# The norm's root in steps between VectorE's long instructions, and five small moves in a two-layer decoder trunk

## The chip, the cores and the metric

The kernel runs on one core of a Trainium2 chip. The metric is the device time of one launch in microseconds. TensorE multiplies, VectorE and ScalarE do the elementwise work and move results out of the accumulators, GpSimd (POOL) issues the DMAs that add to what lies in memory, and SyncE (SP) issues the other DMAs. Each engine works through its own instructions in the order in which the program gives them.

## The reference, cut to what matters

The input x has 512 tokens of 1024 values in float32. Two layers follow; a layer is a gated feed-forward part, a mixing part and a second feed-forward part, each added to x:

```python
for l in range(DEPTH):                                   # 2 layers
    x = x + 0.5 * swiglu(rmsnorm(x, ln_ffn1[l]), w_ffn1_gu[l], w_ffn1_down[l])
    h = rmsnorm(x, ln_mix[l])
    z = h @ w_in[l]                                      # pool, q, k, v, two gates
    ...                                                  # windowed means, attention over 128 tokens
    x = x + (g_pool * a + g_attn * b) @ w_out[l]
    x = x + 0.5 * swiglu(rmsnorm(x, ln_ffn2[l]), w_ffn2_gu[l], w_ffn2_down[l])

def rmsnorm(x, g):  return x * rsqrt(mean(x * x, axis=-1) + 1e-6) * g
def swiglu(h, w_gu, w_down):
    g, u = split(h @ w_gu, 2)                            # 1024 -> 2 x 2816
    return (silu(g) * u) @ w_down                        # 2816 -> 1024
```

The four feed-forward parts (FFNs) hold most of the arithmetic, and the change is in them.

## The kernel before, in words

**Two parts of every number.** Float32 operands are split into a high part that TensorE multiplies at its faster float32 rate and a low part, the rest. A product is three matmuls: high by high, high by low, low by high. ScalarE makes a high part by a rounding copy (`wh` for weights, `xgh`, `more` or `op` for activations), VectorE the low part by a subtraction (`wl`, `xgl`, `more`, `op`). For weights `Weights` (line 168) keeps a plan of tiles of up to 1024 columns: loads run up to 7 tiles ahead, high parts 4 and low parts 3. `prep` (line 295), called once for each tile that is used up, emits the next low part, the next sum of two weight tiles (`add_up`), the next high part and the loads that have a free buffer. A load that is a difference or sum of two tiles is a DMA by SP and an accumulating DMA by POOL.

**Fewer products.** `strassen` (line 551) computes a 2 x 2 block product with seven products instead of eight. Its stages come in the order `a11, s1, s2, a12, s3, s4, a22`. Their activations are combinations of the four blocks: a11 takes B11, s1 takes T1, s2 takes T2, a12 takes B21, s3 takes T3, s4 takes B22, a22 takes T4. The banks A, C and Dd of the accumulators are shared: a11, s2, s3 and a22 add up in A, s1 and s4 in C, a12 in Dd. A stage has two weight tiles (c = 0, 1), and in each two halves of the tokens (q = 0, 1). Behind c = 0 comes a `prep`, behind c = 1 the stage's own step, which moves the bank out, then `settle()`, then another `prep`. `settle` (line 148) emits the low parts that were put off. `mid` names extra work at (stage, c, q): there `settle()` is called and then the entry.

**An FFN** (line 530) has three groups of columns, one of 2 x 384 and two of 2 x 512. In each group two blocks (`block`, line 592) compute gate and up, and `down` (line 765) multiplies by the down weights and adds to x. The first block's results are turned by TensorE through the bank `pt` (`turned`, line 667) in the second block's a11 step, and become down's first operands, for its stages a11 and s1: `made` emitted the high and the low part there. In `down`, the results of a11 and s1 are copied to the tiles `p` and `u` (`aside`) and added to x by POOL's accumulating DMAs (`gathered`); the other stages are added to x by VectorE.

**The norm.** `Norm.sums` (line 480) makes the variance (`rs_v`) and its inverse root by a bit trick and three Newton rounds (`rsqrt`, line 330): two instructions and three times three, on tiles of 128 x 4 values, each of which reads the result of the one before. For an FFN the negative (`nrstd`) follows. The first block of an FFN behind a norm begins its matmuls with the scaled but not yet normed x; the root is needed only by the activations in a12's step and called for in s2's step. At the same time the last two transposed pieces of x come in, and the combinations T2 to T4 are made, by a list of ten pieces of work (`left`, line 522) that `due` takes one by one at entries of `mid` (lines 870 to 875).

**The very first block** is `plain` (line 700): eight weight tiles, in two passes j = 0 and 1 of four (c). VectorE makes the combinations T1 (`first`, four) and T2 to T4 (`other`, four) behind the matmuls of each c, ahead of each `other` ScalarE makes a scaled copy `xg`, and behind j = 0, c = 3 come the root and four Silu activations of the finished pass. The group's second block then runs `strassen`.

All of this is emitted by hand in this order. Since every instruction is recorded at one helper (line 97), the profile's rows are told apart by the tiles' names.

Of the kernel before, what the change touches and what calls it, by code (L numbers as in the profile page):

```python
# [12 lines left out]
I32 = mybir.dt.int32  # L13
# [7 lines left out]
S = 512  # L21
# [87 lines left out]
def trunk(ctx, tc, x0, xT, consts, vecs, rows, w_g4, w_g3, w_d8, w_d6, w_qkv, w_u, w_pool, w_gate, w_br, w_out, out):  # L109
# [36 lines left out]
    unsettled = []  # L146

    def settle():
        while unsettled:
            unsettled.pop(0)()  # L150

# [16 lines left out]
    class Weights:  # L168
# [77 lines left out]
        def add_up(self, upto):  # L246

            while self.summed < len(self.plan):
# [3 lines left out]
                if c["of"] is not None:  # L252
# [12 lines left out]
                    b["uses"] -= 1  # L265
                self.summed += 1
# [8 lines left out]
        def low(self, upto):  # L275
            while len(self.lo) < min(upto, len(self.hi)):
# [6 lines left out]
                c["uses"] -= 1  # L283

# [45 lines left out]
    def rsqrt(y, v):  # L330

        t = sp.tile(list(v.shape), F32, name="rs_t%d" % math.prod(v.shape[1:]))
        nc.vector.tensor_scalar(
            out=y.bitcast(I32), in0=v.bitcast(I32), scalar1=1, scalar2=None, op0=ALU.logical_shift_right
        )
        nc.vector.tensor_scalar(
            out=y.bitcast(I32), in0=y.bitcast(I32), scalar1=-1.0, scalar2=float(0x5F3759DF),
            op0=ALU.mult, op1=ALU.add,
        )
        for _ in range(3):  # L340
            nc.vector.tensor_tensor(out=t, in0=y, in1=y, op=ALU.mult)
            nc.vector.scalar_tensor_tensor(out=t, in0=t, scalar=-0.5, in1=v, op0=ALU.mult, op1=ALU.mult)
            nc.vector.scalar_tensor_tensor(out=y, in0=t, scalar=1.5, in1=y, op0=ALU.add, op1=ALU.mult)
# [4 lines left out]
    class Norm:  # L348
# [92 lines left out]
        def others(self, j, src, xg, scale):  # L441
# [4 lines left out]
            )  # L446
            nc.vector.scalar_tensor_tensor(
                out=t[:, :HT], in0=src[:, :HT], scalar=scale, in1=t[:, HT:], op0=ALU.mult, op1=ALU.subtract
            )
            nc.vector.scalar_tensor_tensor(  # L450
                out=u, in0=t[:, :HT], scalar=-1.0, in1=xg[:, :HT], op0=ALU.mult, op1=ALU.subtract
            )
            split(*self.of(T2, j), t[:, :HT])
# [26 lines left out]
        def sums(self, acc=None, pt=None):  # L480
# [11 lines left out]
            rsqrt(self.rstd, v)  # L492
            if self.halves:
                self.nrstd = xp.tile([P, NB], F32, name="nrstd")
                nc.vector.tensor_scalar(out=self.nrstd, in0=self.rstd, scalar1=-1.0, scalar2=None, op0=ALU.mult)
                return
            hi, lo = sp.tile([P, NB], F32R, name="rs_h"), sp.tile([P, NB], F32, name="rs_l")
# [32 lines left out]
    def ffn(ctx, nm, nxt, last):  # L530
# [20 lines left out]
        def strassen(order, n, sizes, operand, steps, mid={}):  # L551
# [8 lines left out]
            for kind in order:  # L560
# [3 lines left out]
                for c, kn in enumerate(sizes):  # L564
                    wh, wl = (t[:, :kn * n].rearrange("p (k f) -> p k f", k=kn) for t in W.take(kind))
                    for q in range(2):
                        for k in range(kn):
                            ah, al = operand(kind, k0 + k, q)
                            for j, (s, m) in enumerate(((ah, wh), (ah, wl), (al, wh))):
# [3 lines left out]
                                )  # L573
                        if (kind, c, q) in mid:
# [17 lines left out]
        def block(n, i, order, mid):  # L592
# [10 lines left out]
            def s1(pt):  # L603
                tile_["p"] = wide("p")[:, :, :n]
                nc.scalar.copy(out=tile_["p"], in_=pt)

            def s2(pt):
# [3 lines left out]
                if nm.rstd is None:  # L611
                    nm.sums()

            def a12(pt):
                nc.vector.tensor_tensor(out=r, in0=r, in1=pt, op=ALU.add)
# [47 lines left out]
        def made(name, src, n):  # L663
            high(name, src, n)
            low(name)

        def turned(src, i, t, n):
# [10 lines left out]
            elif i == 0:  # L678
                made("a11", pt, n)
                f["a"] = fp.tile([P, 2, S], F32, name="fa")[:, :, :n]  # L680
                nc.vector.tensor_tensor(out=f["a"], in0=pt, in1=f["b"], op=ALU.subtract)
                made("s1", f["a"], n)
# [17 lines left out]
        def plain(n, xt, acc, later):  # L700
# [17 lines left out]

            def other(j):
                xg = temp("xg")  # L720
                nc.scalar.activation(out=xg, in_=part(j + 4), func=AF.Copy, scale=nm.gain[:, j + 4:j + 5])
                nm.others(j, part(j), xg, ngain[:, j:j + 1])
# [4 lines left out]
            for j in range(2):  # L727
                pts = [t[:, q, :n] for t in ((A, C) if j == 0 else (Dd, turn)) for q in range(2)]
                for c in range(4):
# [19 lines left out]
                    if j == 0 and c == 3:  # L749
                        for h, name in enumerate(("r1", "u")):  # L750
                            act.append(wide(name)[:, :, :n])
                            for q in range(2):
                                nc.scalar.activation(
                                    out=act[h][:, q, :], in_=pts[2 * h + q], func=AF.Silu, scale=rs(2 * h + q)
# [10 lines left out]
        def down(n, final):  # L765
# [21 lines left out]
            def aside(t, d, c, pt, name):  # L787
                half = wide(name)
                nc.scalar.activation(out=half, in_=pt, func=AF.Copy, scale=c)
                pend_x.append((x[:, 2 * t:2 * t + 2, d * S:(d + 1) * S], half))  # L790

            def gathered():
                y, half = pend_x.pop(0)
                nc.gpsimd.dma_start(out=y, in_=half, accum_op=ALU.add)
# [3 lines left out]
            def a11(pt):  # L798
                aside(0, 0, 0.5, pt, "p")
# [556 lines left out]
```

## Time and profile before

| | |
|---|---|
| time, median of 3 runs | 1876.44 us (1876.26 to 1877.54) |
| time of the profiled execution | 1876.08 us |
| its span, first to last instruction | 1874.3 us |
| TensorE matmuls | 1854.3 us busy, 99% of the span, 8928 |
| VectorE | 1421.7 us, 76% |
| ScalarE | 1029.8 us, 55% |
| GpSimd | 152.0 us, 8% |
| mean granted TensorE clock | 1.000 |

A row of the timeline gives the start in microseconds from the span's start, the duration, the engine (PE is TensorE, DVE VectorE, ACT ScalarE), the operation, the tiles written and read, the shapes, and in brackets the idle time ahead of it with what ended it. Consecutive rows of one kind are merged (x2). A matmul's row lasts longer than the distance to the next, since matmuls overlap; the pace is read from start to start.

### The profile page before, as it was taken

What the parts mean: (1) busy time and instruction counts of PE and PEld (TensorE: products, weight loads), DVE (VectorE), ACT (ScalarE), POOL (GpSimd) and SP (SyncE); (2) the same over time, 40 slices, a digit from 0 to 9 for tenths busy, and PEclk for the clock granted to TensorE, in tenths of its full rate; (3) what the DMA queues carried; (4) which work ended last, traced back from release to release, by engine and by line L of the source; (5) the groups of instructions that cost most, each with busy time, mean ns of one, the idle gap of its engine ahead of it and who ended that gap; (6) DMA issues with size and microseconds to landing.
All of it is one profiled execution on the core that took longest, in us unless ns stands there. A gap on an engine that the chain in (4) does not pass through costs nothing.

```text
span 1874.3 us, 23990 instructions
## 1 busy us (share of the span) xinstructions
PE 1854.3 (99%) x8928; PEld 1556.8 (83%) x8928; DVE 1421.7 (76%) x1805; ACT 1029.8 (55%) x1517; POOL 152.0 (8%) x176
## 2 busy tenths in 40 slices
PE   9999999999999999999999999999999999999998
PEld 8888888887788789988878898888877887899887
DVE  7878878677563977887898878786675648888877
ACT  6655555645444655555665555565554446646554
POOL 0100101000000001110101111110000001101000
PEclk9999999999999999999999999999999999999999
DMA  8786867322223677687767768763222237677864
GB/s 252 190 243 180 218 175 190 131 79 77 82 90 102 167 201 184 180 227 193 193 167 197 173 180 230 199 183 107 90 68 90 93 87 213 169 192 179 241 180 124
DMA packets 94100, 305.39 MB, mean 163 GB/s; under 512 B 10240, under 2 KB 10496, under 8 KB 93984
## 3 DMA queue, kind: packets, MB, share of 16 engines
q1 hardware_dynamic: 67104, 223.47, 35.1%
q0 software_dynamic: 26736, 80.37, 24.5%
q8 instruction: 70, 1.15, 0.2%
q14 instruction: 46, 0.38, 0.1%
q10 hardware_dynamic: 144, 0.03, 0.0%
HBM read 289.15 MB, written 2.10 MB: 155 GB/s over the span
## 4 chain that ended last, share of the span: by engine, by line
PE 84%; DVE 8%; ACT 5%; issue 2%; DMA 1%; SPq 0%; DVEq 0%; POOL 0%; ACTq 0%
PE mm L97 77%; PE sc L97 4%; DVE wl L97 2%; PE pt L97 2%; ACT wh L97 2%; DVE sums L97 1%; PE pt_pv L97 1%; DVE x L97 1%; DVE more L97 1%; ACT sq L97 1%; ACT xgh L97 1%; ACT xg L97 1%; PE pt_tp L97 1%; DVE xgl L97 0%; ACT s L97 0%
## 5 line engine op out<-in xcount | busy, mean ns | idle before, releaser
L97 DVE TENSOR_TENSOR wl<-raw,wh 128x1024 fp32r<-128x1024 f32 (+3 forms) x443 | 503.8, 1147 | 95.4 <-PE mm L97 57.8
L97 ACT CAST wh<-raw 128x1024 fp32r<-128x1024 f32 (+3 forms) x443 | 433.8, 988 | 249.3 <-PE mm L97 171.8
L97 PE MATMUL mm<-wh,op 128*128 128x512 f32 x1232 | 391.6, 394 | 0.0
L97 PE MATMUL mm<-wh,more 128*128 128x512 f32 (+1 forms) x1104 | 335.0, 374 | 3.0 <-DVE more L97 3.0
L97 PE MATMUL mm<-wl,xgh 128*128 128x512 f32 (+2 forms) x840 | 310.3, 369 | 4.1 <-DVE wl L97 4.0
L97 PE MATMUL mm<-wh,xgh 128*128 128x512 f32 (+2 forms) x840 | 312.8, 372 | 0.9 <-ACT xg L97 0.7
L97 PE MATMUL mm<-wh,xgl 128*128 128x512 f32 (+2 forms) x840 | 310.2, 369 | 0.9 <-DVE xgl L97 0.9
L97 PEld LDWEIGHTS mm<-wh,op 128*128 128x128 f32 x1232 | 231.2, 188 | 48.3 <-DVE op L97 1.7
L97 PE MATMUL mm<-wl,op 128*128 128x512 f32 x616 | 240.6, 391 | 1.6 <-DVE wl L97 1.6
L97 PEld LDWEIGHTS mm<-wh,more 128*128 128x128 f32 x1104 | 204.8, 188 | 34.3 <-DVE more L97 5.0
L97 PE MATMUL mm<-wl,more 128*128 128x512 f32 (+1 forms) x552 | 206.5, 374 | 1.1 <-DVE wl L97 1.1
L97 DVE TENSOR_TENSOR wl<-sums,wh 128x1024 fp32r<-128x1024 f32 (+1 forms) x140 | 159.1, 1137 | 45.8 <-ACT wh L97 27.6
L97 ACT CAST wh<-sums 128x1024 fp32r<-128x1024 f32 (+1 forms) x140 | 136.9, 980 | 89.0 <-DVE sums L97 46.3
L97 POOL DMA_DIRECT2D raw<-in_w_g x92 | 78.5, 854 | 1265.5 <-DMA raw<-in_w_g 743.4
L97 PEld LDWEIGHTS mm<-wl,xgh 128*128 128x128 f32 x840 | 158.1, 188 | 26.9 <-DVE wl L97 6.2
L97 PEld LDWEIGHTS mm<-wh,xgl 128*128 128x128 f32 x840 | 157.9, 188 | 23.4 <-DVE xgl L97 2.2
L97 PEld LDWEIGHTS mm<-wh,xgh 128*128 128x128 f32 x840 | 158.0, 188 | 23.0 <-ACT xg L97 2.0
L97 PEld LDWEIGHTS mm<-wl,op 128*128 128x128 f32 x616 | 115.9, 188 | 26.0 <-DVE wl L97 3.3
L97 PE MATMUL mm<-xgh,wh 128*128 128x512 f32 x320 | 129.3, 404 | 0.0
L97 PE MATMUL mm<-xgl,wh 128*128 128x512 f32 x320 | 125.4, 392 | 0.5 <-DVE xgl L97 0.5
L97 PE MATMUL mm<-xgh,wl 128*128 128x512 f32 x320 | 125.3, 392 | 0.0
L97 PEld LDWEIGHTS mm<-wl,more 128*128 128x128 f32 x552 | 103.7, 188 | 17.6 <-DVE wl L97 2.4
(251 smaller groups left out, 2432.0 us busy)
## 6 DMA issues: line engine op xcount, KB each, us to landing
raw<-in_w_g SPq DMA_DIRECT2D x160, 512.0 KB, 5.2
raw<-in_w_d SPq DMA_DIRECT2D x100, 512.0 KB, 4.5
raw<-in_w_g POOLq DMA_DIRECT2D x64, 512.0 KB, 6.3
raw<-in_w_g SPq DMA_DIRECT2D x77, 384.0 KB, 4.4
raw<-in_w_d POOLq DMA_DIRECT2D x40, 512.0 KB, 5.4
raw<-in_w_gate SPq DMA_DIRECT2D x32, 512.0 KB, 3.2
raw<-in_w_g POOLq DMA_DIRECT2D x28, 384.0 KB, 5.8
raw<-in_w_br SPq DMA_DIRECT2D x16, 512.0 KB, 3.2
```

The lines of the kernel that those rows point to most:

```text
L97: return lambda *args, **kw: self.tc.keep_in_program_order(call(*args, **kw))
```

## The change

The root's twelve instructions become a list (`rsqrt_steps`). For an FFN behind a norm they aren't emitted in a row but put on a list `slow`, from which `tick` takes one behind each deferred low part and each sum of weight tiles, two behind each low part of a weight tile, and one behind each of the three combinations in `Norm.others`. What is left is emitted ahead of a12's addition, or, in `plain`, ahead of the activations. The call moves from s2's step to s1's.

The other moves: the low parts of down's first operands go from the second block's a11 step to entries at s1 (in the first group of all, s2); in down, the copies `aside` go from the ends of a11 and s1 to entries at s1 and s2, and the second accumulating DMA one entry later; in an FFN's first block, the last piece of the list goes from (s3, 1, 1) to (s4, 0, 0), and an empty entry at (a12, 1, 0) settles there; in `plain`, the scaled copies are emitted one `other` ahead, and the activations one c later.

```diff
     def settle():
         while unsettled:
             unsettled.pop(0)()
+            tick()
+
+    def tick(n=1):
+        for _ in range(min(n, len(slow))):
+            slow.pop(0)()
...
 # add_up, behind the sum            +                    tick()
 # low, behind the subtraction       +                tick(2)
 # others, behind each of the three  +            tick()
...
+    def rsqrt_steps(y, v):
+        t = sp.tile(list(v.shape), F32, name="rs_t%d" % math.prod(v.shape[1:]))
+        steps = [
+            lambda: nc.vector.tensor_scalar(
+                out=y.bitcast(I32), in0=v.bitcast(I32), scalar1=1, scalar2=None, op0=ALU.logical_shift_right
+            ),
+            lambda: nc.vector.tensor_scalar(
+                out=y.bitcast(I32), in0=y.bitcast(I32), scalar1=-1.0, scalar2=float(0x5F3759DF),
+                op0=ALU.mult, op1=ALU.add,
+            ),
+        ]
+        return steps + 3 * [
+            lambda: nc.vector.tensor_tensor(out=t, in0=y, in1=y, op=ALU.mult),
+            lambda: nc.vector.scalar_tensor_tensor(out=t, in0=t, scalar=-0.5, in1=v, op0=ALU.mult, op1=ALU.mult),
+            lambda: nc.vector.scalar_tensor_tensor(out=y, in0=t, scalar=1.5, in1=y, op0=ALU.add, op1=ALU.mult),
+        ]
+
     def rsqrt(y, v):
...
+        for step in rsqrt_steps(y, v):
+            step()
...
-            rsqrt(self.rstd, v)
             if self.halves:
                 self.nrstd = xp.tile([P, NB], F32, name="nrstd")
-                nc.vector.tensor_scalar(out=self.nrstd, in0=self.rstd, scalar1=-1.0, scalar2=None, op0=ALU.mult)
+                slow.extend(rsqrt_steps(self.rstd, v))
+                slow.append(lambda: nc.vector.tensor_scalar(
+                    out=self.nrstd, in0=self.rstd, scalar1=-1.0, scalar2=None, op0=ALU.mult
+                ))
                 return
+            rsqrt(self.rstd, v)
...
             def s1(pt):
                 tile_["p"] = wide("p")[:, :, :n]
                 nc.scalar.copy(out=tile_["p"], in_=pt)
+                if nm.rstd is None:
+                    nm.sums()
...
-                if nm.rstd is None:
-                    nm.sums()
 
             def a12(pt):
+                tick(len(slow))
                 nc.vector.tensor_tensor(out=r, in0=r, in1=pt, op=ALU.add)
...
-                made("a11", pt, n)
+                high("a11", pt, n)
                 f["a"] = fp.tile([P, 2, S], F32, name="fa")[:, :, :n]
                 nc.vector.tensor_tensor(out=f["a"], in0=pt, in1=f["b"], op=ALU.subtract)
-                made("s1", f["a"], n)
+                high("s1", f["a"], n)
...
+            xgs = []
+
+            def scaled(j):
+                if j < 4:
+                    xgs.append(temp("xg"))
+                    nc.scalar.activation(
+                        out=xgs[j], in_=part(j + 4), func=AF.Copy, scale=nm.gain[:, j + 4:j + 5]
+                    )
+
             def other(j):
-                xg = temp("xg")
-                nc.scalar.activation(out=xg, in_=part(j + 4), func=AF.Copy, scale=nm.gain[:, j + 4:j + 5])
-                nm.others(j, part(j), xg, ngain[:, j:j + 1])
+                nm.others(j, part(j), xgs[j], ngain[:, j:j + 1])
+                scaled(j + 1)
...
-                    if j == 0 and c == 3:
+                    if j == 0 and c == 1:
+                        scaled(0)
+                    if j and c == 0:
+                        tick(len(slow))
                         for h, name in enumerate(("r1", "u")):
                             act.append(wide(name)[:, :, :n])
                             for q in range(2):
                                 nc.scalar.activation(
-                                    out=act[h][:, q, :], in_=pts[2 * h + q], func=AF.Silu, scale=rs(2 * h + q)
+                                    out=act[h][:, q, :], in_=gates[2 * h + q], func=AF.Silu, scale=rs(2 * h + q)
                                 )
...
             mid = {
-                ("a11", 1, 0): lambda: low("s2"), ("s1", 0, 1): lambda: [low("a12"), gathered()],
-                ("s2", 0, 1): lambda: [high("s3", f["b"], n), gathered()], ("a12", 0, 1): lambda: high("s4", f["c"], n),
+                ("a11", 1, 0): lambda: low("s2"), ("s1", 0, 0): aside, ("s1", 0, 1): lambda: [low("a12"), gathered()],
+                ("s2", 0, 1): lambda: [high("s3", f["b"], n), aside()],
+                ("s2", 1, 0): gathered, ("a12", 0, 1): lambda: high("s4", f["c"], n),
...
+                    if i:
+                        at = "s2" if nm is first and gi == 0 else "s1"
+                        mid[at, 0, 1], mid[at, 1, 1] = lambda: low("a11"), lambda: low("s1")
...
-                            ("s3", 0, 1), ("s3", 1, 1),
+                            ("s3", 0, 1), ("s4", 0, 0),
                         )}
+                        mid["a12", 1, 0] = lambda: None
```

More of the change, by code (lines that the diff above doesn't have):

```diff
@@ L144, in halves @@
         return t.rearrange("p (i t) -> p i t", t=HT)
-    unsettled = []
+    unsettled, slow = [], []
     def settle():
@@ L265, in add_up @@
                     b["uses"] -= 1
+                    tick()
                 self.summed += 1
@@ L283, in low @@
                 c["uses"] -= 1
+                tick(2)
         def parts_of_first(self, k):
@@ L328, in pairs @@
         return [(w[0][:, c], w[1][:, c], *a) for c, a in zip(cols, acts)]
-    def rsqrt(y, v):
[L332 to L343, printed above, removed]
+    def rsqrt_steps(y, v):
[14 more added lines that the diff above has]
+        ]
+    def rsqrt(y, v):
+        for step in rsqrt_steps(y, v):
+            step()
     parts = [xp.tile([P, 2, NB], F32, name=f"part{i}") for i in range(2)]
@@ L446, in others @@
             )
+            tick()
             nc.vector.scalar_tensor_tensor(
@@ L449, in others @@
             )
+            tick()
             nc.vector.scalar_tensor_tensor(
@@ L452, in others @@
             )
+            tick()
             split(*self.of(T2, j), t[:, :HT])
@@ L573, in strassen @@
                                 )
+                            if (kind, c, q, k) in mid:
+                                mid[kind, c, q, k]()
                         if (kind, c, q) in mid:
@@ L661, in low @@
             ops.pop((name, "low"))()
-        def made(name, src, n):
-            high(name, src, n)
-            low(name)
         def turned(src, i, t, n):
@@ L728, in plain @@
                 pts = [t[:, q, :n] for t in ((A, C) if j == 0 else (Dd, turn)) for q in range(2)]
+                gates = gates if j else pts
                 for c in range(4):
@@ L785, in whole, with aside @@
                         nxt.squares(d, b)
-            def aside(t, d, c, pt, name):
-                half = wide(name)
+            def aside():
+                t, d, c, pt, half = pend_x[0]
                 nc.scalar.activation(out=half, in_=pt, func=AF.Copy, scale=c)
-                pend_x.append((x[:, 2 * t:2 * t + 2, d * S:(d + 1) * S], half))
             def gathered():
-                y, half = pend_x.pop(0)
-                nc.gpsimd.dma_start(out=y, in_=half, accum_op=ALU.add)
+                t, d, _, _, half = pend_x.pop(0)
+                nc.gpsimd.dma_start(out=x[:, 2 * t:2 * t + 2, d * S:(d + 1) * S], in_=half, accum_op=ALU.add)
             pend_x = []
             def a11(pt):
-                aside(0, 0, 0.5, pt, "p")
+                pend_x.append((0, 0, 0.5, pt, wide("p")))
                 return flush
             def s1(pt):
-                aside(1, 1, -0.5, pt, "u")
+                pend_x.append((1, 1, -0.5, pt, wide("u")))
                 nc.vector.tensor_tensor(out=f["b"], in0=f["c"], in1=f["b"], op=ALU.subtract)
```

## The prediction

> **What bounds the kernel now.** I read the page's busy times first, then the chain of waits for the pace, then who TensorE waits for, and then the timelines of the stretches in which it waits.
>
> ```profile
> PE 1854.3 (99%) x8928; PEld 1556.8 (83%) x8928; DVE 1421.7 (76%) x1805; ACT 1029.8 (55%) x1517; POOL 152.0 (8%) x176
> ...
> 865.77 32.69 PE mm L97 x144
> 764.44 25.09 PE mm L97 x144
> ...
> PE mm L97 <- DVE wl L97: 6.7, 12, 1.1
> PE mm L97 <- DVE more L97: 3.0, 3, 1.0
> ```
>
> TensorE is the bound: it is busy nearly all of the span, and where nothing holds it a 512-wide matmul starts every 32.69/144 = 0.227 us and a 384-wide one every 25.09/144 = 0.174 us. No part of the change adds or removes a matmul, so it can only move the time by the pauses in this pace. The last two rows name them: TensorE waits for VectorE's low parts, of weights (wl) and of activations (more). The view counts idle time from a modelled end of the matmul before; I measure a pause from start to start instead, less the pace.
>
> **The start of a FFN behind a norm** (layer 0's second FFN; the same code runs at the starts of both FFNs of layer 1, and "more" has three waits with a longest of 1.0 us for the three starts). TensorE, then VectorE, then one row of ScalarE:
>
> ```profile
> 629.00 0.39 PE L97 MATMUL mm<-wl,xgh 128*128 128x512 f32 x1
> 629.70 0.50 PE L97 MATMUL mm<-wh,xgl 128*128 128x512 f32 x1 [0.31 <-DVE xgl L97]
> ...
> 635.20 0.39 PE L97 MATMUL mm<-wl,more 128*128 128x512 f32 x1
> 636.58 0.73 PE L97 MATMUL mm<-wh,more 128*128 128x512 f32 x2 [0.98 <-DVE more L97]
> ...
> 623.30 0.69 DVE L97 TENSOR_TENSOR xgl<-xg,xgh 128x512 fp32r<-128x512 f32 x1 [1.29 <-ACT xgh L97]
> 623.91 2.48 DVE L97 TENSOR_TENSOR wl<-raw,wh 128x1024 fp32r<-128x1024 f32 x2
> 626.31 0.15 DVE L97 TENSOR_TENSOR rs_v<-part 128x4 f32<-128x4 f32 x1
> ...
> 628.88 0.17 DVE L97 TENSOR_SCALAR nrstd<-rstd 128x4 f32<-128x4 f32 x1
> 628.96 0.68 DVE L97 TENSOR_TENSOR xgl<-xg,xgh 128x512 fp32r<-128x512 f32 x1
> ...
> 630.70 1.22 DVE L97 TENSOR_TENSOR sums<-sums,raw 128x1024 f32<-128x1024 f32 x1
> 631.83 0.69 DVE L97 TENSOR_TENSOR more<-more 128x512 fp32r<-128x512 f32 x1
> ...
> 635.84 0.68 DVE L97 TENSOR_TENSOR more<-more 128x512 fp32r<-128x512 f32 x1
> ...
> 625.90 0.62 ACT L97 CAST xgh<-xg 128x512 fp32r<-128x512 f32 x1
> ```
>
> From 626.31 to 629.05 VectorE runs the norm's 14 small instructions (2 for the variance, 11 for the root, 1 for its negative), 0.20 us from start to start, because each reads what the one before wrote. The xgl behind them could have run from 626.52, when its xgh was cast; it ends at 629.64, and TensorE starts at 629.70 instead of 629.23: 0.47 us. At 636.58 TensorE waits again, 636.58 - 635.20 - 0.23 = 1.15 us, for the last T3 low part, which VectorE reached only at 635.84.
>
> **The first block** of the kernel has the other pauses. TensorE, VectorE, ScalarE:
>
> ```profile
> 31.72 0.34 PE L97 MATMUL mm<-wh,xgh 128*128 128x384 f32 x1
> 32.95 0.44 PE L97 MATMUL mm<-wl,xgh 128*128 128x384 f32 x1 [0.90 <-DVE wl L97]
> 33.23 0.34 PE L97 MATMUL mm<-wh,xgl 128*128 128x384 f32 x1
> ...
> 41.23 0.34 PE L97 MATMUL mm<-wh,xgh 128*128 128x384 f32 x1
> 41.63 0.45 PE L97 MATMUL mm<-wl,xgh 128*128 128x384 f32 x1
> ...
> 43.68 0.34 PE L97 MATMUL mm<-wh,xgh 128*128 128x384 f32 x1
> 45.09 0.45 PE L97 MATMUL mm<-wl,xgh 128*128 128x384 f32 x1 [1.07 <-DVE wl L97]
> ...
> 57.16 0.34 PE L97 MATMUL mm<-wh,xgh 128*128 128x384 f32 x1
> 58.64 0.44 PE L97 MATMUL mm<-wl,xgh 128*128 128x384 f32 x1 [1.14 <-DVE wl L97]
> ...
> 31.95 0.95 DVE L97 TENSOR_TENSOR wl<-raw,wh 128x768 fp32r<-128x768 f32 x1
> ...
> 54.03 0.96 DVE L97 TENSOR_TENSOR op<-pt,op 128x768 fp32r<-128x768 f32 x1 [1.50 <-ACT op L97]
> 56.76 0.96 DVE L97 TENSOR_TENSOR op<-fa,op 128x768 fp32r<-128x768 f32 x1 [0.90 <-ACT op L97]
> 57.63 2.69 DVE L97 TENSOR_TENSOR wl<-raw,wh 128x768 fp32r<-128x768 f32 x3
> ...
> 34.77 1.04 ACT L97 ACTIVATE r<-mm,rstd 128x384 f32<-128x384 f32 x2
> ...
> 37.36 0.74 ACT L97 ACTIVATE xg<-op,vec 128x512 f32<-128x512 f32 x1
> ```
>
> Four pauses: 1.23 - 0.17 = 1.06, 0.40 - 0.17 = 0.23, 1.41 - 0.17 = 1.24 and 1.48 - 0.17 = 1.31 us. Behind each pause the next matmul comes 0.11 us late as well (32.95 to 33.23 is 0.28, not 0.17), so a pause costs 0.11 more than its length.
>
> **Part 1: the root in steps.** No instruction is added. The two for the variance move up to s1's step, into the 1.29 us in which VectorE waits for xgh ahead of 623.30: nothing on the path. The 12 steps go out one or two at a time. A step behind a long instruction starts before that ends: rs_v at 626.31 started 0.08 ahead of the end of the wl before it (623.91 + 2.48 = 626.39) and ended at 626.46, so a single step costs 0.08 us; of a pair the second waits for the first and the pair costs 0.08 + 0.20 = 0.28. Counted in the code from s1's step on: xgl's settle 1, wl 2, wl 2, settle 1, wl 2, sums 1, settle 1, wl 2; that is all 12 ahead of a12's step, where what is left would be emptied. Cost 4 x 0.08 + 4 x 0.28 = 1.4 us spread over 9 us, against 2.6 in a row now.
>
> Put back into VectorE's queue: wl 623.99 and 625.42, then the second xgl at 626.84 (two steps behind the wl), done at 627.5 against a need of 629.2, so the first pause goes with 1.7 us to spare. Then wl 627.5, sums 628.95, the first T3 low part 630.2, wl 630.85, sums 632.3.
>
> The new empty entry at a12's second half then settles the last T3 low part ahead of r's addition, not behind it: 633.4 to 634.1. TensorE, earlier by the first pause and its tail (0.47 + 0.11, the tail from the next part's rows), wants it at 635.43 - 0.58 = 634.85. The second pause goes with 0.7 to spare. What is late next? T4's second activation moves from s3's end to s4's start; its low part then comes at about 645.2 and a22 wants it at about 645.6: 0.4 to spare, the tightest place. Gain per start 0.47 + 0.11 + 1.15 + 0.11 = 1.84 us, three starts **5.5 us**. If the pairs cost more than I take, the two thin margins go first; that is the low end, 3 x 0.58 = 1.7 us, where only the first pause is gained.
>
> One rule of the Trainium skill speaks against this part: VectorE: DVE Perf Modes, "The DRAIN you can't avoid" and "Rules for kernel authors", says that the next operation cannot issue until the pipe is empty, and that operations should be made fewer, since chaining changes nothing. By it a step would cost its full length wherever it stands; the overlap at 626.31 above says otherwise. I keep it as a rival below.
>
> **Part 2: the first block.** Three things act there. The root no longer stands ahead of the wl at 31.95, so that wl runs at 29.5 to 30.5; it is needed at 31.72 + 0.17 = 31.9. The xg copies are issued one piece ahead, so that VectorE doesn't wait for the one at 37.36, which stands behind four activations (34.77 on, 2.0 us with those for u). And the activations move to j = 1, c = 0, behind the third of the four combinations. Put back in order with the same durations: the wl that TensorE wants at 40.2 ends at 38.0, and the one it wants at 42.3 ends at 42.0. The activations must have read bank A before the next block writes it at 40.1; they wait for the root's last step at 37.0 and have read A by 38.1. So the first three pauses go: 1.06 + 0.23 + 1.24 + 3 x 0.11 = 2.86 us, the third with 0.3 to spare only; if it isn't gained, 1.5.
>
> The fourth pause: the wl at 57.63 stands behind two low parts that waited 1.50 and 0.90 us for ScalarE's high parts. Those low parts now go out in s2, behind fa and this wl. Without the two waits (2.4 us) and the two instructions (1.9 us) it ends over 2.5 us before it is wanted: 1.31 + 0.11 = 1.4 us. Sum of the block **4.3 us**, low end 1.5 + 1.4 = 2.9.
>
> **Part 3: the downs.** The same move of the two low parts in all other groups takes waits off VectorE where TensorE has no pause, and gains nothing; they are due a whole stage later, and nothing is queued on them in between. The copies of the accumulators (aside) and their accumulating DMAs move back:
>
> ```profile
> 811.93 0.50 PE L97 MATMUL mm<-wl,op 128*128 128x512 f32 x1 [0.41 <-DVE wl L97]
> ...
> 803.17 1.23 DVE L97 SCALAR_TENSOR_TENSOR x<-mm,x 128x1024 f32<-128x1024 f32 x1 [0.84 <-PE mm L97]
> 813.26 1.22 DVE L97 SCALAR_TENSOR_TENSOR x<-mm,x 128x1024 f32<-128x1024 f32 x1
> ...
> 799.09 1.03 ACT L97 ACTIVATE u<-mm 128x1024 f32<-128x1024 f32 x1 [0.25 <-PE mm L97]
> ...
> 801.17 2.04 POOL L97 DMA_DIRECT2D x<-u  x1
> 812.85 0.87 POOL L97 DMA_DIRECT2D raw<-in_w_g  x1 [9.64 <-DVE fa L97]
> ...
> DMA to landing us min/median/max: 7.1/8.5/9.8
> ```
>
> The pause at 811.93 stays: VectorE is without a gap from 803.17, where it waits for TensorE's s2, and its order from there on is unchanged. The copy of s1's bank now stands behind one wh and s3's high part: about 801.3 to 802.3 against 799.09, so its DMA goes at 802.3 against 801.17 and lands at 802.3 + 9.8 = 812.1; the addition that reads it is at 813.26. SP's loads are not passed by it, and POOL's next load (812.85) stays behind it: that load is issued in s2's second prep, the DMA now just ahead of it. Cost 0, cover 1.2 us in the four short downs. The copy of a11's bank moves behind one wh and a12's high part. Of such ScalarE pieces, about 1 us each (799.09: 1.03), three now lie between a11's last matmul and the freed bank, 3.1 us; s1's 18 or 24 matmuls take 4.1 or 5.5 us, and only then does s2 want the bank. Without that cover the price is at most the copy's 1.03 us in each of twelve downs; I take 0.
>
> **Sum:** 5.5 + 4.3 = 9.8 us. The profiled execution took 1876.08 us (span 1874.3), so 1866.3 by its own time; the median of the runs, 1876.44, is 0.36 above it, which makes **1866.6 us**.
>
> **The rivals.** (a) A step costs 0.20 us wherever it stands. (The rule of the Trainium skill's page VectorE: DVE Perf Modes, quoted above, would give this case and its time.) The root then keeps 2.4 us of VectorE against my 1.4, and what comes behind it is 1.0 later: the last T3 low part at 635.1, a pause of 0.3 + 0.11 per start (1.2 us back over three), and the third pause of the first block returns as 0.7 + 0.1. Gain 9.8 - 2.0 = 7.8: 1868.6 us. For it: the steps do follow each other at 0.20. Against it: that is only where each needs the last.
>
> (b) The debt moves on. At a start TensorE gains 1.84 us and VectorE only 1.2 (the 2.6 of the root less the 1.4 of its steps), so the low part that is late next (T4's) holds TensorE instead. Then each start gives 0.58 and the first block its low end: 1.7 + 2.9 = 4.6, 1871.8 us. For it: three margins of 0.3 to 0.7 us. Against: all three would have to fail.
>
> (c) The change does less than it says: the pauses are covered by something that I don't see, such as a load that is not there when TensorE comes earlier. Then about 1876 us. Against it: neither VectorE nor ScalarE shows waits for loads.
>
> (d) Slower: the accumulating DMA of u. If it does get behind POOL's next load at 812.85, it lands near 822.6 and VectorE's addition at 813.26, with the low parts behind it, stands for 9.4 us in each of four short downs: 38 us lost against 9.8 gained, 1904 us. From a landing 9.8/4 = 2.5 us after 813.26 on the kernel is slower than before. For it: the DMA does move back past a prep. Against: the prep that it passes loads nothing.
>
> **Chances.** Forecast 0.64, (a) 0.12, (b) 0.10, (c) 0.07, (d) and other losses 0.07. The forecast's own range is 1864.5 to 1868.5. The range takes in (a) and (b) and leaves out (c) and (d). The 3 us below the forecast are for the pause of 811.93 with its tail in four short downs (0.41 + 0.11 each, 2.1 us), should it shrink along, and 1 us for steps that cost less than I take: **1863.5 to 1872.0**. About 0.2% (3.8 us) can be told from no change: faster 0.86, same 0.07, slower 0.07.
>
> **What would show it.** At the three starts: rs_v ahead of the first xgl, steps singly between long rows, no pause over 0.2 us at xgl and at the last T3 low part, a12's r addition behind it; a pause at a22 would speak for (b), steps 0.16 apart from what follows for (a). In the first block: a wl at 29.5, the activations at about 37, no pause at a11 and a12. In the downs: the same pause as at 811.93, and no addition that waits for a DMA. I am wrong if the three starts together gain less than 2 us, or if the first block does.

## The result and the profile after

The changed kernel takes **1865.28 us** (median of 6 runs, 1864.94 to 1865.74) against 1876.38 us for the kernel before in the same comparison (6 runs, 1875.93 to 1877.54): ratio 0.994, 95% interval 0.9927 to 0.9953. The forecast was 1866.6 us. The profiled execution's span went from 1874.3 to 1862.9 us; 0.4 us of that difference lies behind the last matmul.

The first row is the page's busy times, the last the waits of TensorE for wl with their sum, count and longest (us), both of the kernel after.

```profile
PE 1850.4 (99%) x8928; PEld 1556.6 (84%) x8928; DVE 1417.6 (76%) x1805; ACT 1031.1 (55%) x1517; POOL 152.3 (8%) x176
...
PE mm L97 <- DVE wl L97: 3.6, 9, 0.5
```

The same 8928 matmuls are there; no wait for "more" is left in that view, and the waits for wl fell from 6.7 to 3.6 us, their longest from 1.1 to 0.5. To see where the time went I set the start of each matmul against the start of the same one before, in program order, and read off where the difference grows:

| stretch | grows at (us, before) | gain (us) | forecast |
|---|---|---|---|
| first block | 32.95, 41.63, 45.09, 52.29, 58.64 | 1.17 + 0.34 + 1.35 + 0.21 + 1.41 = 4.5 | 4.3 |
| three FFN starts | 629.70, 964.04, 1560.49 and the 8 us behind each | 1.99 + 2.01 + 2.06 = 6.1 | 5.5 |
| downs | none over 0.12 | | 0 |
| first group of the three later FFNs, second block | 770.97, 1105.30, 1701.75 | 0.10 + 0.10 + 0.08 = 0.3 | 0 |

**A FFN start after**, as a timeline: start, duration, instruction; in brackets the idle time before it and who ended that. VectorE from the first xgl on, then TensorE at the two places that had the pauses.

```profile
618.75 0.69 DVE L97 TENSOR_TENSOR xgl<-xg,xgh 128x512 fp32r<-128x512 f32 x1 [1.01 <-ACT xgh L97]
619.36 0.17 DVE L97 TENSOR_SCALAR rstd<-rs_v 128x4 int32<-128x4 int32 x1
619.43 1.22 DVE L97 TENSOR_TENSOR wl<-raw,wh 128x1024 fp32r<-128x1024 f32 x1
...
622.02 0.15 DVE L97 SCALAR_TENSOR_TENSOR rs_t<-rs_t,rs_v 128x4 f32<-128x4 f32 x1
622.21 0.16 DVE L97 SCALAR_TENSOR_TENSOR rstd<-rs_t,rstd 128x4 f32<-128x4 f32 x1
622.29 0.68 DVE L97 TENSOR_TENSOR xgl<-xg,xgh 128x512 fp32r<-128x512 f32 x1
...
628.79 0.68 DVE L97 TENSOR_TENSOR more<-more 128x512 fp32r<-128x512 f32 x1
629.40 1.21 DVE L97 TENSOR_TENSOR r<-r,mm 128x1024 f32<-128x1024 f32 x1
...
639.84 0.69 DVE L97 TENSOR_TENSOR more<-t,more 128x512 fp32r<-128x512 f32 x1
...
624.45 0.39 PE L97 MATMUL mm<-wl,xgh 128*128 128x512 f32 x1
624.68 0.39 PE L97 MATMUL mm<-wh,xgl 128*128 128x512 f32 x1
...
629.89 0.39 PE L97 MATMUL mm<-wl,more 128*128 128x512 f32 x1
630.12 0.62 PE L97 MATMUL mm<-wh,more 128*128 128x512 f32 x2
```

A single step costs 0.07 us (619.36 to 619.43), a pair 0.27 (622.02 to 622.29). The second xgl ends at 622.97, 1.7 us before 624.68; the last T3 low part at 629.47, 0.65 before 630.12; r's addition stands behind it. TensorE keeps its pace of 0.23 us through both places.

**The first block after**, VectorE, ScalarE and TensorE:

```profile
29.41 0.95 DVE L97 TENSOR_TENSOR wl<-raw,wh 128x768 fp32r<-128x768 f32 x1
...
36.93 0.96 DVE L97 TENSOR_TENSOR wl<-raw,wh 128x768 fp32r<-128x768 f32 x1
37.81 0.48 DVE L97 SCALAR_TENSOR_TENSOR t<-op,ngain,xg 128x256 f32<-128x256 f32 x1
...
40.92 1.82 DVE L97 TENSOR_TENSOR wl<-raw,wh 128x768 fp32r<-128x768 f32 x2
...
36.85 1.05 ACT L97 ACTIVATE r<-mm,rstd 128x384 f32<-128x384 f32 x2
...
40.15 0.33 PE L97 MATMUL mm<-wl,xgh 128*128 128x384 f32 x1
...
42.23 0.33 PE L97 MATMUL mm<-wl,xgh 128*128 128x384 f32 x1
```

The wl come at 30.36, 37.89 and about 41.9, the activations start at 36.85, and matmuls follow each other without a pause. **In the downs** the pause is what it was:

```profile
805.22 0.50 PE L97 MATMUL mm<-wl,op 128*128 128x512 f32 x1 [0.41 <-DVE wl L97]
...
794.94 0.69 DVE L97 TENSOR_TENSOR wl<-raw,wh 128x512 fp32r<-128x512 f32 x1 [1.06 <-ACT u L97]
...
806.55 1.22 DVE L97 SCALAR_TENSOR_TENSOR x<-mm,x 128x1024 f32<-128x1024 f32 x1
```

The addition at 806.55, which reads what u's accumulating DMA has added to, waits for nothing.

### The profile page after: what moved, and what is told of

It is laid out like the page before. It is cut to its first block, busy times and chain, and to the rows that moved or that the text cites. A ratio compares the mean times of both kernels' runs of the same rounds, so it can differ in the third digit from the quotient of the medians.

```text
span 1862.9 us, 24031 instructions
## 1 busy us (share of the span) xinstructions
PE 1850.4 (99%) x8928; PEld 1556.6 (84%) x8928; DVE 1417.6 (76%) x1805; ACT 1031.1 (55%) x1517; POOL 152.3 (8%) x176
## 4 chain that ended last, share of the span: by engine, by line
PE 88%; DVE 6%; ACT 4%; issue 1%; DMA 1%; DVEq 0%; POOL 0%; ACTq 0%
PE mm L97 80%; PE sc L97 4%; PE pt L97 3%; DVE wl L97 2%; ACT wh L97 1%; PE pt_pv L97 1%; DVE sums L97 1%; DVE x L97 1%; ACT xg L97 1%; PE pt_tp L97 1%; ACT sq L97 1%; DVE more L97 0%; ACT xgh L97 0%; DMA x<-p 0%; ACT s L97 0%
```

## The experiments

Each time stands beside the kernel before on the same chip; "behind the change" is how much less an experiment gains over that kernel than the 11.10 us (1876.38 - 1865.28) of the change itself. "Offset" is the start of a matmul less its start in the changed kernel, and its growth tells where the time is lost. Ahead of 12 us, before anything that an edit moves, the profiled executions differ by up to 0.6 us; that part is left out of the readings unless it is named.

**One part alone, one part undone.** First the root in a row again, the other moves kept:

```
-                slow.extend(rsqrt_steps(self.rstd, v))
-                slow.append(lambda: nc.vector.tensor_scalar(...))
+                rsqrt(self.rstd, v)
+                nc.vector.tensor_scalar(out=self.nrstd, ...)
...
+            (nm.sums() back in s2's step)
```

> The changed kernel with only the root put back: its two variance and twelve root instructions stand in a row again, at s2's step in the FFNs behind a norm and behind j = 0, c = 3 in the first block. All other moves stay. Theory of the prediction (the row holds VectorE): each of the three starts gets its first pause back, 0.47 + 0.11 us; the last T3 low part, now ahead of r's addition, stays in time; in the first block the wl at 29.4 comes 2.4 us later, 1.0 + 0.1 us of pause, and the third pause returns with some 0.3 us. Sum 3 x 0.6 + 1.4 = 3.2 us slower than the changed kernel: 1868.5 us. Rival (the other moves make the gain and the root's place makes none): within 0.5 us of the changed kernel, 1865.3 us. Rival (the root's place makes all of it): 1874 or more.

Measured: 1870.23 us (1869.53 to 1870.35) against 1876.29, ratio 0.9967 (0.9954 to 0.998); 5.0 us behind the change. The offset grows by 1.7 us in the first block and by 0.97, 0.99 and 1.05 us at the starts. At a start:

```profile
626.11 0.16 DVE L97 SCALAR_TENSOR_TENSOR rstd<-rs_t,rstd 128x4 f32<-128x4 f32 x1
626.30 0.17 DVE L97 TENSOR_SCALAR nrstd<-rstd 128x4 f32<-128x4 f32 x1
626.38 0.68 DVE L97 TENSOR_TENSOR xgl<-xg,xgh 128x512 fp32r<-128x512 f32 x1
...
629.25 0.68 DVE L97 TENSOR_TENSOR more<-more 128x512 fp32r<-128x512 f32 x1
...
626.47 0.39 PE L97 MATMUL mm<-wl,xgh 128*128 128x512 f32 x1
627.12 0.50 PE L97 MATMUL mm<-wh,xgl 128*128 128x512 f32 x1 [0.26 <-DVE xgl L97]
...
629.74 0.39 PE L97 MATMUL mm<-wl,more 128*128 128x512 f32 x1
629.99 0.73 PE L97 MATMUL mm<-wh,more 128*128 128x512 f32 x2
```

The steps are 0.20 us apart again and xgl is late: 0.42 us with 0.11 behind it. The rest are three small delays of 0.15 us in each start, 1.4 us over the three; the first is at 629.99, where the low part ended at 629.93. At the last T3 low part no more than that is lost even here, because the empty entry at a12 still lets it go ahead of r's addition. So the steps are worth 5.0 us of the 11.1, and most of the second pause belongs to that entry, which the next runs bear out.

The steps alone, all other moves undone (the entry at a12 and the move of T4's activation among them):

```
  (the kernel before, with these of the change only)
+                slow.extend(rsqrt_steps(self.rstd, v))
+                slow.append(lambda: nc.vector.tensor_scalar(...))
+            tick()   (in settle, add_up, others; tick(2) in low; a12 empties the rest)
+                if nm.rstd is None:
+                    nm.sums()   (in s1's step, not in s2's)
```

> The kernel before with only the root in steps, called for in s1's step and handed out behind the low parts and sums; none of the other moves. Theory: at each start the first pause goes (0.58 us), and the last T3 low part still stands behind r's addition, but 1.2 us earlier than before, so that 0.5 + 0.1 of its pause stay: 1.2 to 1.35 us gained per start, about 4 us. In the first block the first pause goes (1.16 us), but the scaled copies still stand behind the activations, so the two pauses behind it grow by nearly as much: 0.2 us gained in all. The pause at 58.64 stays. Sum about 4.2 us faster than before: 1872.2 us. Rival (the root alone does it): 1866. Rival (the root's steps cost as much as the row): 1875 or more.

Measured: 1871.93 us (1871.39 to 1872.71) against 1876.29, ratio 0.9977 (0.9967 to 0.9986). Of the first block's pauses only the one at 31.83 is gone; the others are lost again (0.76, 1.34, 0.20 and 1.41 us by the offset), and at each start 0.65 to 0.95 us at the last T3 low part. The steps alone gain 4.4 us, and the other moves alone 6.1 (the run before this one): together 10.5 of the 11.1, so the parts nearly add up.

The low parts of down's first operands directly behind their high parts again:

```
+        def made(name, src, n):
+            high(name, src, n)
+            low(name)
...
-                high("a11", pt, n)
+                made("a11", pt, n)
-                high("s1", f["a"], n)
+                made("s1", f["a"], n)
...
-                    if i: (the two entries for low("a11") and low("s1"))
```

> The changed kernel with only the low parts of down's first operands put back to the second block's a11 step, right behind their high parts, in all twelve groups. Theory: only the first group pays, where the wl for a12 stands behind the two waits again: 1.3 + 0.1 us slower than the changed kernel, 1866.7 us; the eleven other groups pay nothing. Rival (the low parts matter in every group): 3 us or more slower. Rival (they matter nowhere): within 0.3 us.

Measured: 1866.71 us (1866.41 to 1867.05), ratio 0.9949 (0.9934 to 0.9964). VectorE and TensorE of this run:

```profile
53.84 0.96 DVE L97 TENSOR_TENSOR op<-fa,op 128x768 fp32r<-128x768 f32 x1 [0.90 <-ACT op L97]
54.72 2.69 DVE L97 TENSOR_TENSOR wl<-raw,wh 128x768 fp32r<-128x768 f32 x3
...
54.25 0.34 PE L97 MATMUL mm<-wh,xgh 128*128 128x384 f32 x1
55.72 0.44 PE L97 MATMUL mm<-wl,xgh 128*128 128x384 f32 x1 [1.14 <-DVE wl L97]
```

The fourth pause is back, 1.30 us with 0.10 behind it. Beside it the offset grows by 0.08 to 0.10 us at 764.29, 1096.55 and 1690.80, the three places outside the first block and the starts at which the change had gained 0.1 us, and by 0.33 in the first down (93.24). The last need not be the edit's: the run with extra instructions below, which changes nothing there, loses 0.61 us at the same matmul. So the move is worth its 1.4 us in the first block and 0.1 us in the first group of each later FFN. The copies aside and their DMAs as before:

```
-                ("a11", 1, 0): lambda: low("s2"), ("s1", 0, 0): aside, ...
-                ("s2", 0, 1): lambda: [high("s3", f["b"], n), aside()],
-                ("s2", 1, 0): gathered, ...
+                ("a11", 1, 0): lambda: low("s2"), ...
+                ("s2", 0, 1): lambda: [high("s3", f["b"], n), gathered()], ...
```

> The changed kernel with only down's copies of the accumulators and the accumulating DMAs put back to the ends of a11 and s1. Theory: no pause of TensorE hangs on them: within 0.3 us of the changed kernel, 1865.3 us; the pause at the short downs' s4 (0.57 us, 811.93 in the trace of before) the same in both. Rival (the copies were what the downs gain by): 1 us or more slower.

Measured: 1866.03 us (1865.63 to 1866.21), ratio 0.9945 (0.993 to 0.996). That is 0.8 us behind the change by the medians. The offset grows by 0.16 us at one of the four short downs (1137.48) and at no other down; the rest of its 0.5 us comes from the start-up (0.1 to 0.2) and one place in the attention at 396.29 (0.28), which the edit doesn't touch. So the downs cost next to nothing, and whether the rest is the edit or the spread between runs stays open.

**The two thin margins.** The changed kernel without the empty entry at a12's second half:

```
-                        mid["a12", 1, 0] = lambda: None
```

> The changed kernel without the empty entry at a12's second half, so that the last T3 low part is settled again behind r's addition. Forecast's theory (that place decides the second pause): in the changed kernel's rows r's addition takes 628.79 to 630.0, so the low part would run at 629.92 to 630.6, against 630.12, when TensorE wants it; a pause of about 0.5 us with 0.11 behind it at each of the three starts, 3 x 0.61 = 1.9 us: 1867.2 us. Rival (the steps alone have brought VectorE far enough ahead, the entry does nothing): within 0.3 us of 1865.3.

Measured: 1868.27 us (1867.39 to 1868.59) against 1876.64, ratio 0.9954 (0.9939 to 0.9969). VectorE and TensorE at the first start, then one row of ScalarE at the second:

```profile
629.24 1.22 DVE L97 TENSOR_TENSOR r<-r,mm 128x1024 f32<-128x1024 f32 x1
630.37 0.69 DVE L97 TENSOR_TENSOR more<-more 128x512 fp32r<-128x512 f32 x1
...
631.12 0.73 PE L97 MATMUL mm<-wh,more 128*128 128x512 f32 x2 [0.91 <-DVE more L97]
...
957.96 1.05 ACT L97 CAST wh<-raw 128x1024 fp32r<-128x1024 f32 x1 [0.72 <-DMA raw<-in_w_g]
```

The low part is behind r's addition and TensorE waits. The entry does what the forecast said: at the third start the loss is 0.68 us, as expected (0.61). At the first two it is 1.25 and 1.32, because VectorE is some 0.5 us later there; in this execution ScalarE stood for 0.64 and 0.72 us ahead of the wh in front of its high parts, the second time for a load by the row above; the first wait is put down to VectorE's rstd, which hands that wh no data, so what it was for stays open.

An extra small instruction (a product that nothing reads) behind each of the root's first steps, at the three starts:

```
-                slow.extend(rsqrt_steps(self.rstd, v))
+                def with_spare(i, step):
+                    step()
+                    if spare is not None:
+                        nc.vector.tensor_tensor(out=spare[:, i, :], in0=v, in1=v, op=ALU.mult)
+                slow.extend([lambda ...: with_spare(i, step) for i, step in enumerate(rsqrt_steps(self.rstd, v))])
```

> The changed kernel with an extra small instruction (a product of two 128x4 operands that nothing reads) behind each of the first 11 steps of the root, at the three starts only; it reads nothing that the step wrote. This prices a small instruction that has no need of the one before it. Forecast (what is independent costs 0.07 to 0.08 us): some 8 of them stand ahead of the last T3 low part, 8 x 0.07 = 0.56 us, which the margin of 630.12 - 629.46 = 0.66 us there takes up: 1865.3 to 1865.8 us. Rival (a) (a small instruction costs 0.20 us wherever it stands): 8 x 0.20 = 1.6 us ahead of the last T3 low part, 1.0 us of it as a pause with 0.11 behind it, and the first xgl about 0.2 us late at each start: 3 x 1.3 = 3.9 us, 1869.2 us.

Measured: 1865.45 us (1865.23 to 1866.06) against 1876.64, ratio 0.994 (0.9923 to 0.9956): no loss in the time. VectorE at the first start, where rs_d is the extra one:

```profile
621.61 0.16 DVE L97 TENSOR_SCALAR rstd<-rstd 128x4 int32<-128x4 int32 x1
621.68 0.16 DVE L97 TENSOR_TENSOR rs_d<-rs_v 128x4 f32<-128x4 f32 x1
621.81 0.16 DVE L97 TENSOR_TENSOR rs_t<-rstd 128x4 f32<-128x4 f32 x1
```

An instruction that needs nothing of the one before starts 0.07 us after it (621.61 to 621.68); the next step of the root starts 0.20 us after the one it reads (621.61 to 621.81) with or without one between. So rival (a) falls: 0.20 us is the price of needing the result, not of an instruction. The extra instructions aren't free, they use up the margins: the last T3 low part ends 0.22 us ahead of its matmul (630.91 and 631.13) where it had 0.65, and at T4's first operand each start loses 0.1 to 0.2 us by the offset.

**The two moves in the first block.** The activations back at the end of the first pass, the copies still ahead; then the copies back beside their combinations, the activations still late:

```
-                    if j and c == 0:
+                    if j == 0 and c == 3:
```

> The changed kernel with the first block's activations back at the last piece of the first pass (what is left of the root is emptied there), the scaled copies still one piece ahead. Forecast's theory (the third pause has a margin of only some 0.1 to 0.3 us, and both moves are needed for it): with the activations' gates on ScalarE ahead of the high part of the next weights the wl that TensorE wants at 42.23 ends at about 42.85; a pause of 0.6 us with its tail, 0.3 to 1.3 us lost: 1865.6 to 1866.6, 1866.1 us most likely. Rival (the copies alone remove the third pause): within 0.3 us of 1865.3.

```
-                nm.others(j, part(j), xgs[j], ngain[:, j:j + 1])
-                scaled(j + 1)
+                xg = temp("xg")
+                nc.scalar.activation(out=xg, in_=part(j + 4), func=AF.Copy, scale=nm.gain[:, j + 4:j + 5])
+                nm.others(j, part(j), xg, ngain[:, j:j + 1])
```

> The changed kernel with the first block's scaled copies issued again right ahead of the combination that reads each, the activations still late. Forecast's theory (VectorE waits for the copy that stands behind the activations on ScalarE): the fourth combination starts about 2.5 us later than now, the wl that TensorE wants at 42.23 ends at about 44.3, a pause of 2.1 us with 0.11 behind it: +2.2 us, 1867.5 us. Rival (moving the activations alone removes the third pause): within 0.3 us of 1865.3.

Measured: 1866.26 us (1866.16 to 1866.55) and 1867.77 us (1867.23 to 1869.53) against 1876.64, ratios 0.9944 (0.993 to 0.9959) and 0.9954 (0.9939 to 0.9969). The run with the activations back, TensorE:

```profile
42.99 0.44 PE L97 MATMUL mm<-wl,xgh 128*128 128x384 f32 x1 [0.28 <-DVE wl L97]
```

And the run with the copies back, VectorE, ScalarE and TensorE:

```profile
40.67 0.48 DVE L97 SCALAR_TENSOR_TENSOR t<-op,ngain,xg 128x256 f32<-128x256 f32 x1 [2.34 <-ACT xg L97]
...
39.89 0.75 ACT L97 ACTIVATE xg<-op,vec 128x512 f32<-128x512 f32 x1
...
44.17 0.45 PE L97 MATMUL mm<-wl,xgh 128*128 128x384 f32 x1 [1.43 <-DVE wl L97]
```

Both moves are needed to be rid of the pause at 42.23: with the copies ahead alone 0.45 us of it is left, and with the late activations alone it is 1.59 us, more than the 1.24 of the kernel before; each has 0.11 behind it and 0.20 more at 49.12.

**The price of the slower rival (d).** The changed kernel with u's accumulating DMA behind POOL's next load:

```
-                ("s2", 1, 0): gathered, ("a12", 0, 1): ...
+                ("a12", 0, 0): gathered, ("a12", 0, 1): ...
```

> The changed kernel with the accumulating DMA of u issued a little later, in a12's first piece, so that on POOL it stands behind the next load of weights. This prices the slower rival (d). In the changed kernel's rows that load goes out at 806.71 in a short down; u's DMA would go at about 807.3 and land 8.4 to 9.8 us later, near 816, and VectorE's addition that reads it, at 806.55 now, would stand for some 9 us with the low parts of weights behind it. Rival (d)'s price: four short downs at 8.6 to 9.4 us, 34 to 38 us, and in the four long ones, where the load goes at 206.47 and the addition at 210.36, up to 5 us each, 20 us more: 1900 to 1923 us. Other reading (the wait is hidden by VectorE's lead, or the load is issued early enough): under 10 us, below 1875 us.

Measured: 1927.98 us, one run, against 1876.80. POOL and VectorE at the first short down, the row of VectorE's waits, and TensorE behind the long wait:

```profile
92.17 0.90 POOL L97 DMA_DIRECT2D raw<-in_w_g  x1 [8.63 <-DVE x L97]
92.74 1.55 POOL L97 DMA_DIRECT2D x<-u  x1
...
103.79 1.23 DVE L97 SCALAR_TENSOR_TENSOR x<-mm,x 128x1024 f32<-128x1024 f32 x1 [8.62 <-DMA x<-u]
...
DVE x L97 <- DMA x<-u: 46.0, 7, 8.6
...
109.79 1.05 PE L97 MATMUL mm<-wh,op 128*128 128x512 f32 x2
110.65 0.63 PE L97 MATMUL mm<-wl,op 128*128 128x512 f32 x1
```

It costs 62.7 us. The mechanism is the one described and the size is above the range: 9.7 to 11.1 us in each short down, not 8.6 to 9.4, and 3.4 to 7.0 us in each long down. What the range left out is TensorE's clock: behind the long wait its matmuls start every 0.43 us instead of 0.23 (two of them from 109.79 to 110.65). The granted clock is 0.51 from 105.0 to 112.2 us, and 1.00 from 90.0 to 97.5 and again from 112.2 on. Each matmul at the lower clock costs 0.20 us more, up to 2.8 us for the 14 in this down. The changed kernel stays clear of it by one prep.

**A faster version.** In the downs above VectorE stands idle for 1.06 us ahead of the wl at 794.94. First the low part of s3 goes into that gap; then, in the mixing before a FFN, one preparation of weights goes ahead of the last settling as well:

```
-                low("s3")                     (in s2's step)
-                ("s2", 0, 1): lambda: [high("s3", f["b"], n), aside()],
+                ("s2", 0, 1): lambda: [high("s3", f["b"], n), low("s3"), aside()],
```

> The changed kernel with the low part of s3's operand of down issued one entry earlier, directly behind its high part. In the changed kernel's rows VectorE has a gap there (the wl at 794.94 shows 1.06 us of idle time ahead of it), and TensorE pauses 0.57 us at 805.22 and 0.16 us at 809.82 for what VectorE does later, the same in all four short downs. Theory (VectorE's order is what delays that wl, and the gap can take the low part): 4 x (0.57 + 0.11 + 0.16 + 0.11) = 3.8 us: 1861.5 us. Rival (the low part waits for its high part in the gap and moves nothing, or another wait takes the pause's place): within 0.5 us of 1865.3.

```
+                        W.prep()              (ahead of the last settle() of the mixing)
...
-        W.prep()
```

> The kernel before with one more move: at the end of each group of the mixing before a FFN one preparation of weights goes ahead of the last settling, so that its wl runs in the gap ahead of the first xgl. TensorE pauses 0.62 us at 605.90 and 0.49 us at 615.18 for wl at the two FFN starts behind a mixing. Theory: the first pause goes with its 0.11 us, the second in part, 0.7 to 1.2 us each: 1.4 to 2.4 us below the run with the low part of s3 alone, 1859 to 1860 us. Rival (the pause at 605.90 is for the xgh that the wl now delays): no gain against that run.

Measured: 1860.33 us (1859.95 to 1861.23) and 1858.49 us (1857.26 to 1859.74) against 1876.87; ratios 0.9912 (0.9898 to 0.9927) and **0.99** (0.9883 to 0.9916). The first, VectorE in the same down:

```profile
793.11 0.96 DVE L97 TENSOR_TENSOR op<-fb,op 128x768 fp32r<-128x768 f32 x1
794.17 0.69 DVE L97 TENSOR_TENSOR wl<-raw,wh 128x512 fp32r<-128x512 f32 x1
...
1131.28 1.23 DVE L97 SCALAR_TENSOR_TENSOR x<-mm,x 128x1024 f32<-128x1024 f32 x1 [0.51 <-DMA x<-p]
```

It gains 5.4 us over the change where 3.8 was expected, but only half of the 3.8 came where it was expected: by the offset the four short downs give 1.9 us. The pause is gone in two of them (805.22 and 1731.73), shrank from 0.57 to 0.30 us in the third (1137.48) and stayed in the first (0.56 us, at 93.24). In the third, VectorE now waits for p's accumulating DMA (the row at 1131.28); in the first, the same addition stands for 0.77 us, and the profile doesn't name what for. The other 3.4 us come from the ends of the first three FFNs: 0.19, 0.19, 0.39 and 0.38 us at 323.80, 327.20, 337.24 and 341.56, and the same at 918 to 947 and 1250 to 1268. I had not counted them; that they hang on the same debt of VectorE is likely, but no run separates them.

The second adds 1.8 us by the medians. TensorE's pause at 605.90 is gone (0.62 and 0.11 us by the offset, and the same at 1532.41); the one at 615.18, expected to go in part, stayed (0.49 us). What bounds the downs next shows in its trace:

```profile
800.93 1.23 DVE L97 SCALAR_TENSOR_TENSOR x<-mm,x 128x1024 f32<-128x1024 f32 x1 [1.05 <-DMA x<-p]
...
804.22 0.50 PE L97 MATMUL mm<-wl,op 128*128 128x512 f32 x1 [0.68 <-DVE wl L97]
...
DVE x L97 <- DMA x<-p: 1.4, 2, 1.1
```

VectorE comes so early that in two of the downs it waits for p's accumulating DMA, and in this one TensorE's pause is back, longer than it was. The two moves would have to be followed by an earlier DMA; it was not tried.

## Why the prediction was right

**Part 1** was right in mechanism and 0.6 us short. A single step costs 0.07 (forecast 0.08) and a pair 0.27 (0.28). The margins came out as worked: 1.7 us at the second xgl, 0.65 at the last T3 low part (0.7). T4's low part ends at 640.53; in the run with the root in a row its counterpart came just in time for the matmul that starts at 641.00 here, so the spare is 0.47 (0.4). The mis-sized term is the gain per start, 1.84 us, which measured 1.99 to 2.06: I had counted the two long pauses with their tails (1.84, measured 0.58 + 1.25) and not the delay of 0.15 us between them, at the first T3 operand (632.57 before), which goes as well.

**Part 2** was right: 4.5 against 4.3 us. The order that I put together by hand held to within 0.15 us (wl at 37.89 and 41.9 for 38.0 and 42.0, activations at 36.85 for 37.0), and the margin of 0.3 us at the third pause was real: the two runs that undo one move each lose it. Left out was the pause at 52.29, 0.21 us. The fourth pause measured 1.41 (1.42).

**Part 3** was right in the downs: no growth there, the pause of 805.22 unchanged, no addition that waits for a DMA. That the two low parts gain nothing outside the very first group was 0.3 us off: in the first group of each later FFN their move gained 0.1 us, and both runs without the move lose 0.08 to 0.11 us at just these places.

**The sum** was 9.8 us, and 11.0 by matmul starts (11.1 by the medians). The 1.2 us are the three delays of 0.15 (0.5), the pause at 52.29 (0.2), the three gains of 0.1 by the low parts (0.3) and the rounding of the rest.

**The rivals.** (a) is refuted by the run with extra instructions. (b) did not come. At its place, T4's first operand, 0.1 to 0.2 us per start are lost in the runs with the root in a row and with extra instructions, so that margin is as thin as forecast; the 0.7 to 1.3 us per start of the run without the entry at a12 come from the order of two instructions, not from (b). (c) was right in one detail: against it I said that ScalarE shows no waits for loads, and before the change it shows none for weights (at the very start it waits 1.1 and 0.6 us for other inputs). In the changed kernel two of 1.2 us in all have appeared, under which TensorE does not pause, and in the run without the entry at a12 one of 0.72 us did add to a loss. (d) has the price and the place described, and the DMA stays ahead of the load.

## What to carry to other kernels

A chain of small dependent instructions is cheap when each is put behind a long independent instruction: a single step then costs the engine a third of its price in a row (0.07 of 0.20 us), and the engine's debt, not the chain's length, decides what the matmuls see. Work out each pause from start to start with what follows it, then move the late consumer's operand ahead of anything that can wait; here one empty entry that only reorders was worth 2.7 us. Before a copy or DMA is moved, find the next instruction of its queue that waits for something: one place further back cost 63 us.

## What was not expected of the hardware

- A matmul that has to wait, however briefly, costs more than its wait. In the run with the root in a row the low part ended at 629.93, 0.04 us ahead of when its matmul would have started at the pace (629.74 + 0.23 = 629.97); that matmul started at 629.99, and the sum of its delay and that of the one behind it was 0.15 us. Such delays show only as a "0.73" where its neighbours have 0.62.
- TensorE's clock fell to half behind a wait of some 7 us. In the run with u's DMA behind the load it starts no matmul between 97.52 and 105.16; from 105.0 to 112.2 its granted clock is 0.51, and a 512-wide matmul starts every 0.43 us, not every 0.23. The wait so costs more than its length, and the mean clock of that execution is 0.986.
- On VectorE an independent small instruction between two dependent ones took no time (621.61 to 621.81 with one between, 0.20 us, as without). The Trainium skill's page VectorE: DVE Perf Modes, "The DRAIN you can't avoid", has the flush as a start-to-start gap and adds that an operation which is not held starts earlier; these rows agree with the addition (0.07 us), not with "DRAIN happens regardless" in its "Rules for kernel authors". The prediction had taken up the rule without the addition.
- With TensorE earlier, loads of weights and accumulating DMAs come into sight. ScalarE waits for loads of weights in the changed kernel and in every run of the experiments (0.4 us in all with the steps alone, 0.8 to 3.3 us in the others, 1.7 at most at once), and VectorE for p's DMA in the two fastest (up to 1.1 us); the kernel before shows neither.
